# Weight sums staged in the tiles of later gated outputs, later landing estimates in the planner, gate scalings open to ScalarE, and earlier reloads of the first gated tiles

## The chip, the cores and the metric

The kernel runs on one core of a Trainium2 chip. The metric is device time in microseconds, from the first to the last work of one execution; the figure compared is the median of several runs. The engines are named as the profile names them: PE is TensorE (the matrix engine), PEld its weight loads, DVE is VectorE, ACT is ScalarE, POOL is GpSimd, and SP is the engine on whose queue nearly all transfers are issued.

## The reference

One layer of a mixer over 512 frames of 2048 features, all in float32. Both head groups read the same input through one projection; their gated outputs are concatenated, projected back, added to the input and normalised.

```python
proj = einsum('btd,dc->btc', h, w_in)                    # 512 x 2048 by 2048 x 8320
rw   = _token_shift(proj[..., :RWKV_COLS], shift_mu)     # y + mu * (y_prev - y)
hg   = proj[..., RWKV_COLS:]
# RWKV-7 group, 16 heads of 64
a = sigmoid(a0 + ad @ a_up)
k = k * (1.0 + (a - 1.0) * k_a)
o = _rwkv7_scan(r, decay, k, v, -kk, kk * a)             # a state 64 x 64 for each head
o_rwkv = (group_norm(o) + bonus) * silu(z_r)
# HGRN2 group, 8 heads of 128
log_f = logaddexp(log_lb, log1p(-lb) + log_sigmoid(f_raw))
k = (1.0 - lb) * sigmoid(-f_raw)
o_hgrn = rms_norm(_hgrn2_chunkwise(q, log_f, k, i)) * g_norm_w * silu(z_h)
y = einsum('btc,cd->btd', concatenate([o_rwkv, o_hgrn]), w_out)   # 512 x 2048 by 2048 x 2048
h = _layer_norm(ALPHA * h + y, ln_w, ln_b)
```

## The kernel before

**The large products.** A float32 factor is split into a rounded part and the rest (tiles xh and xl of the input, wh and wl of the weights). Each product of a 128x128 and a 128x512 tile is then three matmuls: high by high, high by low, low by high (`three`, L520). There are 3,852 of these matmuls; the text calls them large matmuls. Weights come in transfers of 128x1024 into tiles wr, two buffers of them; each half is split by ACT (wh, a rounding copy) and DVE (wl, the subtraction, L378), into three buffers. One such half serves 12 large matmuls of a projection.

**The projections.** `ORDER` lists 57 units of 48 large matmuls and two of 192 (w, k, r, v, z for the RWKV group, q, f, g, i for HGRN2). PE walks that list. Between its large matmuls the short matmuls of the heads are put in.

**The heads.** For each two RWKV heads' groups there is a preparation, an inversion of triangular 32x32 blocks (`rwkv_invert`, some 60 short DVE instructions and five long transposes on inv and big tiles), a fold, and a scan over eight chunks. In a scan step PE multiplies the state bd by q ("mix<-bd,q"), DVE subtracts the result from zz (L378), PE multiplies zz by q ("mix<-zz,q"), and DVE updates bd. A finished head gives a gated tile g; twelve of the sixteen are written to DRAM (spill), and pairs of them are read back and combined (`put_gated`, `token_sums`).

**The output product.** Its first 512 columns and its last 512 are computed directly; columns 512 to 1536 by seven products of half-size blocks instead of eight, which need sums of weight blocks (`weight_sums`, L1319) and sums over token halves of the gated tiles. The weight sums are made early: sixteen pieces of 128x1024 are read from w_all, four subtractions on DVE turn a piece into its four sums, and the result is written to sums_w in DRAM and read again near the end. Two threads do this, one with each of the two inv tiles. The inversion asks for both inv tiles too (`room(inv=2)`).

**What sets the order.** No order is written out by hand apart from `ORDER`. A planner (`Plan`, L91) keeps an estimated clock for each engine and for the transfers. It walks PE's large matmuls; after each (`pump`) it offers every thread its next step, and issues it if its operands are estimated to be there and its engine is near. What it issues is then the program order on that engine; on the chip each engine runs its own instructions strictly in that order and waits on semaphores. An estimate that is too early therefore costs a wait on the chip, with all that stands behind it on that engine. For a transfer `fetched` (L161) assumes that it lands 1.8 us after its bytes have passed. An operation with several ways (`Op`) is given to the engine that is estimated to end it first.

**Around the end.** `split_gated` splits a gated tile into gh and gl, in the buffers of xh and xl, which the last projection (z7) gives back a piece at a time; `reload` issues its read from spill first. `begin_out` is a hook that runs within z7: it reloads four tiles and, from the second quarter on, splits one in each quarter. `residual` reads the input rows (x_r), `fetch_norm` the weights of the last normalisation, `bring` the stored token sums, and `extra` opens two more buffers of two t tiles for weights.

## Time and profile before

| what | value |
|---|---|
| time, median of 3 runs | 1014.86 us (1014.38 to 1015.51) |
| the profiled execution: its own time | 1015.35 us |
| the profiled execution: span, first to last instruction | 1013.5 us |
| PE busy | 1005.8 us (99%), 7081 matmul records |
| PE weight loads busy | 830.8 us (82%) |
| DVE busy | 864.2 us (85%) |
| ACT busy | 507.0 us (50%) |
| POOL busy | 43.0 us (4%) |
| granted TensorE clock | 1.00 (2.4 GHz) in every slice |
| mean DMA rate | 160 GB/s, 349 GB/s in the first slice |

A matmul's end in the profile is modelled: a matmul of 128x512 is shown with 0.39 us, while the next one starts 0.23 us after it. So the busy share of PE is no measure of lost time. What shows lost time is the distance from one start to the next in the list of instructions in order of time, and the square brackets behind an instruction, which tell how long its engine sat idle before it and what ended that. The rows further below are of that kind. A label such as "main<-xl,wh" names the tile written and the tiles read, without buffer numbers.

### The profile page before, as it was taken

To read this page: it belongs to the slowest core of one execution; us is meant where nothing else is said; L and a number is where in the kernel's file an instruction comes from. 1 tells how busy PE (TensorE), PEld (TensorE's weight loads), DVE (VectorE), ACT (ScalarE), POOL (GpSimd) and SP (SyncE) were. 2 spreads that over 40 slices of the span, in tenths; PEclk is the share of its full clock that TensorE was granted. 3 is DMA by queue.
4 is the path that set the end of the run, shared out by engine and by line. 5 is a ranking of instruction groups with operands and counts; after the bars stand their busy time and mean duration, and the time that the engine had idled before them with its cause. 6 is when DMAs were issued, how large, how long until landed. Compare 5 with 4: busy or idle time off the path is not lost.

```text
span 1013.5 us, 18887 instructions
## 1 busy us (share of the span) xinstructions
PE 1005.8 (99%) x7081; PEld 830.8 (82%) x7081; DVE 864.2 (85%) x1894; ACT 507.0 (50%) x963; POOL 43.0 (4%) x78
## 2 busy tenths in 40 slices
PE   9999999999999999999999999999999999999997
PEld 8888888888888888888888888888888878888886
DVE  7688689967898998888989987888999887998867
ACT  5557335344646335535673456636343555466531
POOL 0000000000010001002000010020001001000001
PEclk9999999999999999999999999999999999999999
DMA  9666664443455453235555422346463248797633
GB/s 349 234 208 212 220 218 142 130 136 86 140 146 182 109 151 95 64 100 151 151 180 160 111 87 85 90 140 174 140 182 118 70 139 252 221 314 239 206 125 127
DMA packets 80492, 161.74 MB, mean 160 GB/s; under 512 B 11408, under 2 KB 38288, under 8 KB 80400
## 3 DMA queue, kind: packets, MB, share of 16 engines
q1 hardware_dynamic: 79968, 159.61, 51.2%
q8 instruction: 56, 0.92, 0.4%
q10 hardware_dynamic: 432, 0.92, 0.2%
q14 instruction: 36, 0.29, 0.1%
HBM read 130.48 MB, written 30.02 MB: 158 GB/s over the span
## 4 chain that ended last, share of the span: by engine, by line
PE 91%; DVE 4%; DMA 3%; issue 1%; SPq 1%; ACT 1%; DVEq 0%; ACTq 0%
PE main L525 69%; PE mix L354 9%; PE mix L525 8%; PE main L1390 3%; PE main L354 2%; DMA far<-ksq 1%; DVE wl L378 1%; DVE inv L378 1%; SPq L332 1%; DMA t<-w_all 1%; DVE t L378 1%; DVE xl L378 0%; DMA g<-x_r 0%; PE mix L1341 0%; DMA t<-far 0%
## 5 line engine op out<-in xcount | busy, mean ns | idle before, releaser
L525 PE MATMUL main<-xl,wh 128*128 128x512 f32 x848 | 333.2, 393 | 0.0
L525 PE MATMUL main<-xh,wl 128*128 128x512 f32 x848 | 333.1, 393 | 0.0
L525 PE MATMUL main<-xh,wh 128*128 128x512 f32 x848 | 332.9, 393 | 0.0
L368 ACT ACTIVATE wh<-wr 128x512 fp32r<-128x512 f32 x285 | 177.7, 627 | 166.3 <-PE main L525 120.0
L378 DVE TENSOR_TENSOR wl<-wr,wh 128x512 fp32r<-128x512 f32 x285 | 193.9, 681 | 28.8 <-ACT wh L368 24.8
L525 PEld LDWEIGHTS main<-xh,wl 128*128 128x128 f32 x848 | 159.3, 188 | 32.5
L525 PEld LDWEIGHTS main<-xl,wh 128*128 128x128 f32 x848 | 159.3, 188 | 32.4
L525 PEld LDWEIGHTS main<-xh,wh 128*128 128x128 f32 x848 | 159.3, 188 | 32.2
L525 PE MATMUL main<-wh,xh 128*128 128x512 f32 x194 | 76.2, 393 | 0.1
L378 DVE TENSOR_TENSOR inv<-inv 128x256 f32<-128x256 f32 (+10 forms) x184 | 64.5, 355 | 13.6 <-DMA inv<-w_all 10.1
L525 PE MATMUL main<-wh,xl 128*128 128x512 f32 x194 | 76.0, 392 | 0.0
L525 PE MATMUL main<-wl,xh 128*128 128x512 f32 x194 | 75.9, 391 | 0.0
L525 PEld LDWEIGHTS main<-wh,xh 128*128 128x128 f32 x194 | 36.4, 188 | 8.1 <-DVE t L391 0.5
L525 PEld LDWEIGHTS main<-wl,xh 128*128 128x128 f32 x194 | 36.4, 188 | 7.4
L525 PEld LDWEIGHTS main<-wh,xl 128*128 128x128 f32 x194 | 36.4, 188 | 7.3
L378 DVE TENSOR_TENSOR inv<-inv,inv 64x30 f32<-64x30 f32 (+14 forms) x120 | 38.5, 321 | 2.7
L368 ACT ACTIVATE t<-mix 64x128 f32<-64x128 f32 (+3 forms) x71 | 18.4, 262 | 41.3 <-DVE zz L378 23.9
L378 DVE TENSOR_TENSOR t<-t,tot 128x256 f32<-128x256 f32 x96 | 37.9, 416 | 0.3
L369 ACT ACTIVATE t<-main,om 128x512 f32<-128x512 f32 x33 | 22.2, 685 | 29.4 <-PE main L525 22.3
L391 DVE SCALAR_TENSOR_TENSOR bd<-mix,pc,bd 64x64 f32<-64x64 f32 x112 | 31.7, 283 | 5.3 <-PE mix L354 3.0
L368 ACT ACTIVATE q<-t 128x256 f32<-128x256 f32 (+1 forms) x51 | 21.9, 446 | 25.7 <-DVE t L378 25.5
L391 DVE SCALAR_TENSOR_TENSOR t<-main,pr,t 128x511 f32<-128x511 f32 x33 | 24.3, 744 | 5.8 <-ACT t L369 5.5
(320 smaller groups left out, 1607.7 us busy)
## 6 DMA issues: line engine op xcount, KB each, us to landing
wr<-w_all SPq DMA_DIRECT2D x142, 512.0 KB, 3.9
inv<-w_all SPq DMA_DIRECT2D x16, 512.0 KB, 5.0
sums_w<-inv SPq DMA_DIRECT2D x16, 512.0 KB, 5.1
q<-head SPq DMA_DIRECT2D x14, 448.0 KB, 5.6
far<-ksq SPq DMA_DIRECT2D x22, 256.0 KB, 4.2
t<-w_all SPq DMA_DIRECT2D x20, 256.0 KB, 4.9
t<-spill SPq DMA_DIRECT2D x17, 256.0 KB, 4.2
far<-q SPq DMA_DIRECT2D x8, 512.0 KB, 5.1
```

The source lines that it names most:

```text
L332: nc.sync.dma_start(o, i)
L354: return Op([("pe", cost, lambda: pe.matmul(o, l, r, start=start, stop=stop, **kw))], [l, r], [o], mode=("narrow", l.shape[0], 32 if m <= ...
L368: return "act", cost, lambda: sc_e.activation(o, i, f, scale=scale)
L369: return "act", cost, lambda: sc_e.activation(o, i, f, scale=scale, bias=bias)
L378: return dve_op([a, b], o, lambda: dve.tensor_tensor(o, a, b, f), base=base or 0.16 if o.shape[0] < P and size(o) == C and o.tensor.name i ...
L391: return dve_op([a, b], o, lambda: dve.scalar_tensor_tensor(o, a, s, b, f1, f2), per=0.00113, base=0.085 if o.shape[0] == P and size(o) > ...
L525: pe.matmul(ps, l, r, start=first and i == 0, stop=last and i == 2)
L1390: pe.matmul(pss[a], *ops, start=k == 0 and low == of == 0, stop=k == KT - 1 and low == 1)
```

## The change

The planner's function for transfers takes the delay as an argument, and six callers pass a larger one: 4.0 us for the reload of a stored gated tile that is to be combined, for the weight sums, for x_r and for the last normalisation's weights, 3.6 us for the reload of a gated tile before its split, 4.5 us for the stored token sums. The loads of weights into wr and into the t tiles keep 1.8 us. The planner also adds 0.09 us to PE's clock for a large matmul that follows a 128x128 one of the heads.

The weight sums move from one inv tile of 128x1024 for each of two threads to two g tiles of 128x512 each. A piece is read by two transfers of 128x512 instead of one of 128x1024, and written by two instead of one; the same four subtractions are done. The inv tiles are then free for the inversion from the start. The normalisation's weights come in eight transfers instead of four.

Three scalings by values of one per row (one of the RWKV preparation, two of the HGRN2 gates) may go to ACT as well as to DVE (`affine`). In the program, the eight of the preparation and eight of the sixteen of the gates do. A hook `ahead_of_out` reloads gated tiles within z6, one projection earlier than before, where four t tiles are free.

```diff
-    def fetched(self, tile, size):
+    def fetched(self, tile, size, late=1.8):
         self.clock["dma"] = max(self.clock["dma"], self.clock["sp"]) + size * 128 / 360e3
-        self.ready[tile.tensor.name] = (self.clock["dma"] + 1.8, "dma")
+        self.ready[tile.tensor.name] = (self.clock["dma"] + late, "dma")
...
+    def affine(o, a, s1, s2=0.0):
+        if isinstance(s2, float):
+            f = lambda: dve.tensor_scalar(o, a, s1, None, ALU.mult)
+            w = act_way(o, a, AF.Copy, s1)
+        else:
+            f = lambda: dve.tensor_scalar(o, a, s1, s2, ALU.mult, ALU.add)
+            w = act_way(o, a, AF.Identity, s1, s2)
+        return Op([w, ("dve", 0.07 + size(o) * banked(a), f)], [a], [o])
...
-            plan.clock["pe"] += n / 2400 + 0.0145 + plan.turn(("main",))
+            plan.clock["pe"] += n / 2400 + 0.0145 + plan.turn(("main",)) + (0.09 if plan.mode[0] == "whole" else 0.0)
...
-                    plan.fetched(r, 4 * T)
+                    plan.fetched(r, 4 * T, 4.0)
...
-        yield ts(a, a, hcol(HKA, p), hcol(HOKA, p), ALU.mult, ALU.add)
+        yield affine(a, a, hcol(HKA, p), hcol(HOKA, p))
...
-            yield ts(f, f, olb[:, h : h + 1], lbm[:, h : h + 1], ALU.mult, ALU.add)
-            yield ts(k, k, olb[:, h : h + 1], None, ALU.mult)
+            yield affine(f, f, olb[:, h : h + 1], lbm[:, h : h + 1])
+            yield affine(k, k, olb[:, h : h + 1])
...
     def weight_sums(first):
-        yield room(inv=1)
-        w = take("inv", [P, 4, QT // 2])
+        yield room(g=2)
+        ws = [take("g", [P, 2, QT // 2]) for _ in range(2)]
+        w = [w_[:, i] for w_ in ws for i in range(2)]
         for i in range(first, 2 * NPAIRS, 2):
             m, h = divmod(i, 2)
-            yield lambda: plan.clock["sp"] <= plan.clock["pe"] + 0.2
-            send(w, w_all[nsent + i].rearrange("p (a c) -> p a c", a=4))
-            plan.fetched(w, 4 * HALF)
+            cs = slice(h * QT // 2, (h + 1) * QT // 2)
+            raw = w_all[nsent + i].rearrange("p (a c) -> p a c", a=4)
+            for j, w_ in enumerate(ws):
+                yield lambda: plan.clock["sp"] <= plan.clock["pe"] + 0.2
+                send(w_, raw[:, 2 * j : 2 * j + 2])
+                plan.fetched(w_, 2 * HALF, 4.0)
             for o, a, b in ((0, 1, 0), (1, 3, 1), (3, 3, 0), (2, 2, 3)):
-                yield tt(w[:, o], w[:, a], w[:, b], ALU.subtract)
-            yield lambda: by_now(w)
-            yield lambda: plan.clock["sp"] <= plan.clock["pe"] + 0.2
-            send(sums_w[:, :, m, h * QT // 2 : (h + 1) * QT // 2].rearrange("a p c -> p a c"), w)
-            there = plan.busy[w.tensor.name] = (plan.clock["sp"] + 4.5, "dma")
-            yield lambda: there[0] <= plan.clock["pe"]
-        drop(w)
+                yield tt(w[o], w[a], w[b], ALU.subtract)
+            for j, w_ in enumerate(ws):
+                yield lambda: by_now(w_) and plan.clock["sp"] <= plan.clock["pe"] + 0.2
+                send(sums_w[2 * j : 2 * j + 2, :, m, cs].rearrange("a p c -> p a c"), w_)
+                plan.busy[w_.tensor.name] = (plan.clock["sp"] + 5.5, "dma")
+            there = plan.clock["sp"] + 5.5
+            yield lambda: there <= plan.clock["pe"]
+        drop(*ws)
...
                 send(gated[k], spill[SPILL.index(k)])
-                plan.fetched(gated[k], 4 * T)
+                plan.fetched(gated[k], 4 * T, 3.6)
...
         send(r, sums_a[m : m + some, i, :, half].rearrange("m p c -> p m c"))
-        plan.fetched(r, 2 * T * some)
+        plan.fetched(r, 2 * T * some, 4.5)
...
+    def ahead_of_out(j):
+        if plan.free("t", 4):
+            reload(min(len(asked) + 1, 4))
+
...
-            ps = proj(unit(), begin_out if (name, j) == ("z", NPAIR - 1) else None)
+            near = {("z", NPAIR - 1): begin_out, ("z", NPAIR - 2): ahead_of_out}
+            ps = proj(unit(), near.get((name, j)))
...
             send(xr, x_r[t, :, d * T : d * T + T])
-            plan.fetched(xr, 4 * T)
+            plan.fetched(xr, 4 * T, 4.0)
...
-        for d in range(4):
-            c = slice(d * T, d * T + T)
-            send(w[:, :, c], ln_wb[None, :, c].to_broadcast([P, 2, T]))
-            plan.fetched(w, 8 * T)
+        for d in range(8):
+            c = slice(d * T // 2, d * T // 2 + T // 2)
+            send(w[:, :, c], ln_wb[None, :, c].to_broadcast([P, 2, T // 2]))
+            plan.fetched(w, 4 * T, 4.0)
             now = plan.clock["pe"]
-            yield lambda: plan.clock["pe"] > now + 5.0
+            yield lambda: plan.clock["pe"] > now + 6.0
```

The first place is SP's queue around the start of z7. The reads of gated tiles are "t<-spill", the loads of weights "wr<-w_all". Before:

```order
L332 DMA wr_8569<-w_all 128x1024
L332 DMA wr_8681<-w_all 128x1024
L332 DMA wr_8753<-w_all 128x1024
L332 DMA t_8776<-spill 128x512
L332 DMA t_8778<-spill 128x512
L332 DMA t_8780<-spill 128x512
L332 DMA t_8782<-spill 128x512
L332 DMA t_8852<-spill 128x512
L332 DMA wr_8872<-w_all 128x1024
```

The same stretch of SP's queue in the changed program:

```order
L332 DMA wr_8570<-w_all 128x1024
L332 DMA wr_8663<-w_all 128x1024
L332 DMA t_8683<-spill 128x512
L332 DMA t_8715<-spill 128x512
L332 DMA wr_8747<-w_all 128x1024
L332 DMA t_8762<-spill 128x512
L332 DMA wr_8862<-w_all 128x1024
L332 DMA t_8883<-spill 128x512
L332 DMA t_8914<-spill 128x512
```

Five reads in a row have become two, one and two, with loads of weights between them, and the first two stand one load earlier.

The second place is SP's queue at the end of the first 512 output columns, where x_r and the t tiles of `extra` are loaded. Before:

```order
L332 DMA g_9527<-x_r 128x512
L332 DMA g_9533<-x_r 128x512
L332 DMA g_9550<-x_r 128x512
L332 DMA g_9557<-x_r 128x512
L332 DMA t_9553<-w_all 128x512
L332 DMA t_9554<-w_all 128x512
L332 DMA wr_9582<-w_all 128x1024
L332 DMA t_9574<-w_all 128x512
L332 DMA t_9575<-w_all 128x512
```

The same stretch in the changed program:

```order
L332 DMA g_9568<-x_r 128x512
L332 DMA g_9573<-x_r 128x512
L332 DMA g_9582<-x_r 128x512
L332 DMA g_9587<-x_r 128x512
L332 DMA t_9592<-w_all 128x512
L332 DMA t_9593<-w_all 128x512
L332 DMA t_9596<-w_all 128x512
L332 DMA t_9597<-w_all 128x512
L332 DMA wr_9618<-w_all 128x1024
```

The second pair of t tiles now stands ahead of the load into wr instead of behind it.

The third place is DVE's queue where the inversion of the first group begins (the transposes inv<-big). Before:

```order
L378 TENSOR_TENSOR wl_1682<-wr_1532,wh_1681 128x512
L378 TENSOR_TENSOR t_1016<-t_1016,tot_1326 128x16x16
L378 TENSOR_TENSOR tot_1325<-tot_1326 128x16
L427 COPY q_1320<-t_1016 128x8x32
L404 STREAM_TRANSPOSE inv_1698<-big_772 32x1024
L378 TENSOR_TENSOR wl_1711<-wr_1589,wh_1710 128x512
```

And in the changed program, where the instructions on g tiles are weight sums:

```order
L378 TENSOR_TENSOR g_271<-g_272,g_271 128x256
L378 TENSOR_TENSOR wl_1088<-wr_976,wh_1087 128x512
L414 STREAM_TRANSPOSE inv_1082<-big_765 32x1024
L378 TENSOR_TENSOR wl_1109<-wr_1019,wh_1108 128x512
L414 STREAM_TRANSPOSE inv_1082<-big_765 32x1024
L378 TENSOR_TENSOR wl_1126<-wr_1019,wh_1125 128x512
L378 TENSOR_TENSOR inv_1083<-inv_1082 64x30
L378 TENSOR_TENSOR inv_1082<-inv_1082,inv_1083 64x30
L378 TENSOR_TENSOR inv_1083<-inv_1082 64x58
L378 TENSOR_TENSOR inv_1082<-inv_1082,inv_1083 64x29x2
L378 TENSOR_TENSOR g_272<-g_272,g_271 128x256
```

The inversion of the first group begins 20 weights' halves earlier (its first transpose moves from ahead of large matmul 662 to ahead of 423), and weight sums stand within it and after it; before, the last of them stood ahead of it.

## Rows read from the trace of the kernel before

**Rows 1.** The chain that ended last, an undisturbed piece: start, duration, what.

```profile
57.20 16.11 PE main L525 x71
```

**Rows 2.** Instructions in order of time around 820 us: start, duration, instruction [idle before].

```profile
812.64 3.83 SPq L332 DMA_DIRECT2D t<-spill  x5
...
818.18 0.63 ACT L368 ACTIVATE xh<-t 128x512 fp32r<-128x512 f32 x1 [1.70 <-PE mix L354]
...
818.84 0.69 DVE L378 TENSOR_TENSOR xl<-t,xh 128x512 fp32r<-128x512 f32 x1 [1.33 <-ACT xh L368]
...
819.82 0.39 PE L525 MATMUL main<-xh,wl 128*128 128x512 f32 x1
...
820.90 0.47 DVE L378 TENSOR_TENSOR zz<-zz,mix 64x128 f32<-64x128 f32 x2
...
821.23 0.71 PE L354 MATMUL mix<-zz,q 128*128 128x128 f32 x4 [1.01 <-DVE zz L378]
```

**Rows 3.** The stored gated tiles' transfers between 800 and 895 us.

```profile
DMA to landing us min/median/max: 2.9/4.5/7.4
```

**Rows 4.** In order of time from 880 to 885 us.

```profile
880.75 0.69 DVE L391 SCALAR_TENSOR_TENSOR q<-g,main 128x512 f32<-128x512 f32 x1 [1.35 <-DMA g<-x_r]
...
882.78 0.33 SPq L332 DMA_DIRECT2D wr<-w_all  x1
...
883.20 0.86 SPq L332 DMA_DIRECT2D t<-w_all  x2
...
884.24 0.39 PE L525 MATMUL mix<-wh,xh 128*128 128x512 f32 x1
...
884.61 0.50 PE L525 MATMUL mix<-wl,xh 128*128 128x512 f32 x1
...
884.94 0.40 PE L525 MATMUL mix<-wh,xl 128*128 128x512 f32 x1
```

**Rows 5.** In order of time from 889 to 891 us.

```profile
889.12 0.63 ACT L368 ACTIVATE wh<-t 128x512 fp32r<-128x512 f32 x1 [1.74 <-DMA t<-w_all]
...
889.95 0.40 PE L525 MATMUL mix<-wh,xh 128*128 128x512 f32 x1
...
890.54 0.50 PE L525 MATMUL mix<-wl,xh 128*128 128x512 f32 x1 [0.19 <-DVE wl L378]
```

**Rows 6.** In order of time at 570 and at 830 us, PE alone.

```profile
569.81 0.39 PE L525 MATMUL main<-wl,xh 128*128 128x512 f32 x1
...
570.45 0.47 PE L354 MATMUL mix<-ksq,ones_r 128*128 128x512 f32 x1 [0.25 <-DVE ksq L378]
...
829.57 0.39 PE L525 MATMUL main<-wh,xl 128*128 128x512 f32 x1
...
830.02 0.50 PE L525 MATMUL main<-wh,xh 128*128 128x512 f32 x1
```

**Rows 7.** Costliest groups, shapes apart: busy us, mean ns | idle before.

```profile
L378 DVE TENSOR_TENSOR inv<-inv 128x256 f32<-128x256 f32 x64 | 26.0, 421 | 11.0 <-DMA inv<-w_all 10.1
...
L388 DVE TENSOR_SCALAR t<-t,half 128x512 f32<-128x512 f32 x8 | 4.3, 536 | 0.0
...
L369 ACT ACTIVATE t<-main,om 128x512 f32<-128x512 f32 x33 | 22.2, 685 | 29.4 <-PE main L525 22.3 <-PE main L1390 7.0
```

**Rows 8.** Transfers by line: count, size, median us to landing.

```profile
inv<-w_all SPq DMA_DIRECT2D x16, 512.0 KB, 5.0
...
t<-w_all SPq DMA_DIRECT2D x20, 256.0 KB, 4.9
...
g<-x_r SPq DMA_DIRECT2D x16, 256.0 KB, 5.6
```

**Rows 9.** Busy time by stretch: PE, PEld, DVE, ACT, POOL; clock, DMA.

```profile
160.00:200.00 40.00, 40.00 (x221) 32.91 (x220) 38.29 (x96) 16.33 (x35) 0.16 (x1) 1.00 0.51 149
```

**Rows 10.** Who waited for whom, whole span: total, times, longest (us).

```profile
DVE inv L378 <- DMA inv<-w_all: 10.1, 7, 3.3
```

**Rows 11.** One line's instructions, the long transposes: first and last start.

```profile
L404 DVE STREAM_TRANSPOSE inv<-big x8: 1962/2020/2042, 164.1 to 727.0; 32x1024 f32<-32x1024 f32 x8
```

## The prediction

> **What bounds the kernel now.** The page comes first. PE is busy for 1005.8 of 1013.5 us, but a matmul's end is modelled there, so this share can't say how much is lost. The chain of waits comes second: an undisturbed piece of it has 71 large matmuls in 16.11 us, 0.227 us each [rows 1]. 3,852 of them make 874 us; the rest of PE's time is the short matmuls of the heads and the two ends of the span. The reader is to see that PE is the bound from 5 us on, and that nothing else can set the time unless it makes PE wait. The third view is therefore the list of instructions in order of time, where a distance between two starts above 0.227 us, with no short matmul between, is lost time. I looked for all distances that stand out and found five places, worth 2.7 us together:
>
> - At 820 us PE starts a large matmul at 819.82 and the next instruction at 821.23 [rows 2]: 1.41 - 0.23 = 1.18 us lost. PE waited for zz from DVE. Five reads from spill were issued in a row from 812.64 on. ACT's split of the first one began only at 818.18 after 1.70 us idle; DVE's subtraction of that split stood idle 1.33 us for it, and zz was queued behind it until 820.90. The profile names PE as what ACT waited for. I take it for the transfer: 818.18 - 812.64 = 5.5 us, and such reads took 2.9 to 7.4 us there [rows 3].
> - At 884 us: 884.24 to 884.61 is 0.37, and the next distance is 0.33, so 0.14 + 0.10 = 0.24 us. DVE had stood 1.35 us for x_r at 880.75, and the weights' subtractions were queued behind that [rows 4].
> - At 890 us: 889.95 to 890.54 is 0.59, so 0.36 us, and 0.10 for the distance after it as above: 0.46 us. ACT had stood 1.74 us for a t tile of weights [rows 5]. That load had stood in SP's queue behind one into wr and was issued at 883.20 [rows 4].
> - At 570 and at 830 us: distances of 0.64 and 0.45 [rows 6], so 0.41 + 0.22 and 0.10 after each: 0.83 us, let us say 0.8.
>
> 1.18 + 0.24 + 0.46 + 0.8 = 2.7. So 2.7 us, 0.27%, is all that better order can return, and a change of 0.2% is 2.03 us, about what a measurement of this kernel can tell from no change.
>
> **The change part by part.** *What PE executes.* The order shows the same 3,852 large and 1,648 short matmuls on PE, in 124 separate groups of short ones instead of 122, and the same kinds of groups. Two more breaks cost at most two such distances after a break, 2 x 0.10 = 0.2 us [rows 4], and at least nothing, because the short matmuls themselves are the same; I take 0, as the 0.10 was read after a wait. The last 100 instructions of PE and DVE are of the same kinds in the same order, so the tail keeps its time.
>
> *Reload delay and the hook in z6.* The first two reads from spill now stand one load of weights earlier on SP, and the other three are spread among the loads. Between the load in front of which they stand and the first split on ACT lie three halves of weights, each good for 12 large matmuls: 3 x 12 x 0.227 = 8.2 us, against a landing of 4.5 us in the median and 7.4 at most [rows 1, 3]. The wait of 1.33 us on DVE goes, and with it 1.18 us on PE. What is late next there: DVE has the subtraction of the first split directly before zz again. By the order the split may begin when 12 matmuls of z7 are done; 0.63 on ACT and 0.69 on DVE take it 1.3 us further, with the two zz instructions (0.47) 1.8 us [rows 2]. PE needs zz after nine large matmuls and a pair of short ones, at 9 x 0.227 = 2.0 us plus that pair. It fits, with few tenths of a us to spare.
>
> *x_r taken to land 4.0 us after its bytes.* DVE's additions on x_r are placed later in its queue, and the weights' subtractions ahead of them. The planner had 1.8 and a transfer of 256 KB at 360 KB a us, 0.7, so 2.5 us; now 4.7; the rows have 5.6 in the median [rows 8]. Up to 0.9 us of the 1.35 can stay, and that is less than a split tile's lead of 12 x 0.227 = 2.7 us. I count the 0.24 as gone, and nothing as the other bound.
>
> *The second pair of t tiles.* It passes one load into wr in SP's queue. That load was issued at 882.78, the pair at 883.20, and with 0.43 for each issue the pair could now stand right behind the first pair, some 2 us earlier [rows 4]. ACT's wait was 1.74 us [rows 5], so 0.46 us go; the bound below is 0, if SP is held elsewhere. The load into wr comes 0.9 us later for it, under the cover of the other wr tile.
>
> *Weight sums in g tiles.* 64 subtractions of 421 ns stay, 27 us of DVE [rows 7]. 32 transfers become 64: 32 more issues of 0.43 us, 14 us of SP, spread over some 200 us. Each half waits on SP for its sums, and loads into wr are queued behind it; while one wr tile is read the other is loaded, and a tile lasts 24 large matmuls, 5.4 us. While that cover holds it costs nothing; without it, PE stands as long as SP did beyond it. The inversion of the first group, which began at 164.1 us [rows 11], begins 239 large matmuls earlier, 239 x 0.227 = 54 us, thus near 110 us. Nothing waits for it sooner: the fold that follows stands at large matmul 891 instead of 903. So it brings nothing to PE by itself.
>
> *Scalings on ACT.* Sixteen of 536 ns leave DVE, 8.6 us; ACT takes sixteen of about 685 ns (its nearest row with a factor per row), 11 us [rows 7]. DVE takes some short copies back. ACT is half idle, so at worst each holds a split of weights for 0.69 us, within the 2.7 us lead; at best DVE's freed time takes away the waits at 570 and 830 us. I count 0, between 0 and 0.8 us of gain.
>
> *The normalisation's weights* come in eight issues instead of four and are used 80 us later: nothing.
>
> **The sum.** 1.18 + 0.24 + 0.46 = 1.88 us. Of the profiled execution's own time, 1015.35 us (its span and 1.85 us around it), 1013.5 us are left. The median of the runs stands 0.49 us below that execution, so the forecast for it is 1014.86 - 1.9 = 1013.0 us, 0.18% less.
>
> **The rivals.**
>
> *All five waits go.* For it speaks that the planner's clock is nearer to the rows for six kinds of transfers and for PE's own turn, so DVE is held less in general. Against it: the waits at 570 and 830 us have no transfer of those kinds beside them. 1014.86 - 2.7 = 1012.2 us.
>
> *New waits as large as the old.* Nearly every engine's queue is in another order; the loads into wr, most of all transfers, keep their 1.8 us. Five places of thin margin can be five others. Net of 0.4 us: 1014.5 us.
>
> *Slower: DVE held within the inversion.* From 160 to 200 us DVE was busy for 38.29 of 40 us, with the inversion and no weight sums, and PE lost nothing [rows 9]. Now weight sums stand among the inversion's instructions. A sum that waits for its load holds DVE in order, and in so full a stretch nothing is left to catch up with: the weights' subtractions come late by as much, and PE stands. Such waits were 10.1 us in seven, 1.44 us each, the longest 3.3 [rows 10], all ahead of the inversion. Three pieces of sums fall into the inversion by the order. Three waits of 1.44 are 4.3 us: 1013.0 + 4.3 = 1017.3 us. It decides from waits of 3.9 us together on (1.9 gained and 2.0 lost). Against it: the sums are now taken to land at 4.7 us, near their 5.0 [rows 8].
>
> By the page "DMA: Bandwidth & Descriptors" of the Trainium skill (section "Anatomy of one DMA"), a transfer costs a fixed 2.0 us and its bytes at 436 KB a us, and its "Rules for kernel authors" ask for large transfers; halving the pieces then pays 2.0 us twice, and if the two parts came one after the other, three pieces would be late by 6 us and this rival would end near 1019 us. This trace speaks against that: 256 KB land in 4.9 us, issued in pairs, and 512 KB in 5.0 [rows 8], so the halves lie beside each other and I leave the rival its price by rows.
>
> **How the numbers follow.** The forecast has 0.46, all waits gone 0.20, as many new ones 0.19, the slower one 0.15. Faster by over 0.2% means under 1012.8 us: all of the second case and some 0.18 of the first, whose own range is 1012.2 to 1013.9; together 0.38. Slower means over 1016.9: the 0.15. The same: 0.47. The range runs from 1011.3 (all waits gone, and half a us of the spread of the runs shown, with small waits that I did not list) to 1016.8 us, where the smaller part of the slower case is in.
>
> **What would show it.** After the change, around z7, DVE's subtraction on xl should have no idle time before it and the zz matmuls should follow at 0.23 us; DVE should not stand for x_r when the first 512 columns end, nor ACT for a t tile of weights. The inversion's first transpose should begin near 110 us, with PE's starts 0.227 us apart beside it. The prediction is wrong if PE's distances between 105 and 165 us show waits of a us or more, or if the three places keep theirs.

## The result and the profile after

| | median | runs shown | ratio to before, 95% interval |
|---|---|---|---|
| before, same chip | 1015.18 us | 1014.38 to 1016.79 (4) | |
| changed | 1021.31 us | 1017.05 to 1022.90 (4) | 1.0053 [1.0034, 1.0072] |
| changed, measured again (e1) | 1023.08 us | 1020.40 to 1023.59 (5) | 1.0071 [1.0059, 1.0083] |

The change costs 6 to 8 us. The forecast was 1013.0 us in a range of 1011.3 to 1016.8: wrong by sign. The executions also lie further apart than those of before, so one trace isn't enough: the first trace is of the shortest execution (1017.05 us), that of e1 of one of 1020.40 us.

What was forecast for PE at the three places came true. In the first trace of the changed kernel, in order of time, DVE's subtraction of the reloaded tile has no idle time before it, and PE's next distance comes after 823.36 - 822.99 = 0.37 us, so 0.14 us are lost where it was 1.18 [rows 2]:

```profile
822.30 0.68 DVE L378 TENSOR_TENSOR xl<-t,xh 128x512 fp32r<-128x512 f32 x1
...
822.99 0.39 PE L535 MATMUL main<-xh,wl 128*128 128x512 f32 x1
...
823.36 0.71 PE L354 MATMUL mix<-zz,q 128*128 128x128 f32 x4
```

The signs that I had named for the other two came true in part: DVE still stands 0.39 us for x_r where it was 1.35 [rows 4], and ACT 1.16 us for a t tile where it was 1.74 [rows 5]. PE no longer stands for either:

```profile
883.03 0.69 DVE L401 SCALAR_TENSOR_TENSOR q<-g,main 128x512 f32<-128x512 f32 x1 [0.39 <-DMA g<-x_r]
...
886.93 1.99 ACT L368 ACTIVATE wh<-t 128x512 fp32r<-128x512 f32 x3 [1.16 <-DMA t<-w_all]
```

The losses are elsewhere. Here is the list of PE in the execution of e1, the changed kernel once more: every start with over 0.4 us idle before it, from 100 us on, and the start ahead of it. The first one has no releaser: "issue" is idle time in which PE waited for nothing that the profile shows. The group that it cuts in two takes 165.82 - 162.86 = 2.96 us to the next large matmul (next fence), where such a group alone takes 158.64 - 157.96 = 0.68, so 2.28 us are lost. The other distances lose 1.10, 1.42, 0.77 and 0.57 us (over 0.23 us behind a large matmul, 0.31 ahead of mix<-q,t), and 0.32 and 0.42 us more stand right behind 598 and at 531 us; 6.9 us together. Some 2.3 of the 2.7 us of before are gone, so 4.6 us are left; the two executions differ by 1020.40 - 1015.35 = 5.05 us, and the rest is in distances that lose 0.3 us or less.

```profile
165.58 0.31 PE L354 MATMUL mix<-inv,inv 32*32 32x32 f32 x11 [2.06 <-issue]
...
208.35 0.39 PE L535 MATMUL main<-xh,wl 128*128 128x512 f32 x1
209.67 0.47 PE L354 MATMUL mix<-ksq,ones_r 128*128 128x512 f32 x1 [0.94 <-DVE ksq L378]
...
573.41 0.39 PE L535 MATMUL main<-wh,xh 128*128 128x512 f32 x1
575.05 0.47 PE L354 MATMUL mix<-ksq,ones_r 128*128 128x512 f32 x1 [1.26 <-DVE ksq L378]
...
597.73 0.39 PE L535 MATMUL mix<-wl,xh 128*128 128x512 f32 x1
598.82 1.21 PE L354 MATMUL mix<-q,t 128*32 128x48 f32 x64 [0.70 <-DVE q L378]
...
871.23 0.39 PE L535 MATMUL main<-wh,xh 128*128 128x512 f32 x1
872.03 0.63 PE L359 MATMUL mix<-cst,t 128*128 128x128 f32 x4 [0.41 <-DVE t L378]
```

What the first stand is, is seen from what PE did before it (same trace). Three groups of 64 short matmuls stand within 6 us, the last two back to back, and PE stops within the third, after 53 of 64. (The trace has 3,229 records of short matmuls for the program's 1,648, so most leave two.)

```profile
157.96 0.75 PE L354 MATMUL mix<-big 32*32 32x32 f32 x64
158.64 0.50 PE L535 MATMUL main<-wh,xh 128*128 128x512 f32 x1
...
162.04 0.89 PE L354 MATMUL mix<-q,t 128*32 128x48 f32 x64
162.86 0.65 PE L354 MATMUL mix<-inv,inv 32*32 32x32 f32 x53
...
165.82 0.50 PE L535 MATMUL main<-wh,xl 128*128 128x512 f32 x1
```

In the kernel before, the two groups of the inversion (mix<-big and mix<-inv,inv) stood at 213 and 218 us, alone. They are 55 us earlier because the inversion is: its first transpose starts at 105.6 us, where it was 164.1 [rows 11], and I had forecast 110. That puts them among the three groups of mix<-q,t, which moved as well, but the other way: from 139, 147 and 156 us to 143, 162 and 174 us.

The page's section on queues has what runs out there:

```profile
q8 instruction: 56, 0.92, 0.4%
```

These are PE's instructions: 56 transfers of 16,384 bytes, one for every 250 or so of its 14,162 matmuls and weight loads. In large matmuls such a piece lasts some 28 us; 128 short matmuls and their weight loads use one up in 1.5 us (0.82 and 0.68 us for the two groups).

That PE waits for such a piece can be counted. With its waits on semaphores PE has 14,294 records, 917,504 / 14,294 = 64 bytes each, so 256 make a piece. From 20 us on, the traces of this case have six stands for 'issue' of 0.9 us or more, and all of them lie at the border of a piece: in e1, e4, e5, e6 and e14 PE stops after record 1,985, in e4 too, whose order is another, and a second time in e14, at 611 us, after record 8,897, which is 1,985 + 27 x 256. In all six PE goes on 1.2 to 1.4 us after the last transfer of that queue before it has ended (in e1 it runs from 163.22 to 164.14 us, and PE goes on at 165.58).

### The profile page after: what moved, and what is told of

Its sections match the earlier page's. It is cut to its first block, busy times and chain, and to the rows that moved or that the text cites. A ratio compares the mean times of both kernels' runs of the same rounds, so it can differ in the third digit from the quotient of the medians.

```text
span 1015.2 us, 18915 instructions
## 1 busy us (share of the span) xinstructions
PE 1006.5 (99%) x7081; PEld 831.8 (82%) x7081; DVE 861.7 (85%) x1894; ACT 512.8 (51%) x963; POOL 42.4 (4%) x78
## 4 chain that ended last, share of the span: by engine, by line
PE 92%; DVE 3%; DMA 2%; ACT 1%; issue 1%; SPq 0%; DVEq 0%; ACTq 0%
PE main L535 68%; PE mix L354 10%; PE mix L535 9%; PE main L1405 3%; PE main L354 2%; DMA q<-far 1%; DVE wl L378 1%; DMA g<-w_all 1%; PE mix L1356 0%; DMA wr<-w_all 0%; DVE t L378 0%; SPq L332 0%; DVE g L378 0%; DVE big L414 0%; DVE inv L378 0%
## 5 line engine op out<-in xcount | busy, mean ns | idle before, releaser
L535 PE MATMUL main<-wh,xh 128*128 128x512 f32 x168 | 66.1, 394 | 0.0
L535 PE MATMUL main<-wl,xh 128*128 128x512 f32 x168 | 65.6, 391 | 0.0
L535 PE MATMUL main<-wh,xl 128*128 128x512 f32 x168 | 65.6, 390 | 0.0
L378 DVE TENSOR_TENSOR inv<-inv 64x30 f32<-64x30 f32 (+14 forms) x120 | 38.3, 319 | 2.4
L535 PEld LDWEIGHTS main<-wh,xl 128*128 128x128 f32 x168 | 31.5, 188 | 6.6
L535 PEld LDWEIGHTS main<-wh,xh 128*128 128x128 f32 x168 | 31.5, 188 | 6.5
L535 PEld LDWEIGHTS main<-wl,xh 128*128 128x128 f32 x168 | 31.6, 188 | 6.3
L369 ACT ACTIVATE t<-main 128x512 f32<-128x512 f32 x31 | 18.1, 595 | 23.1 <-PE main L535 23.0
```

The source lines that it names most:

```text
L369: return "act", cost, lambda: sc_e.activation(o, i, f, scale=scale, bias=bias)
L378: return dve_op([a, b], o, lambda: dve.tensor_tensor(o, a, b, f), base=base or 0.16 if o.shape[0] < P and size(o) == C and o.tensor.name i ...
L535: pe.matmul(ps, l, r, start=first and i == 0, stop=last and i == 2)
```

## The experiments

The kernel before measured 1014.51 to 1015.28 us beside them, and each ratio is to that. Theories A to G are named in the expectations.

**e1_again** is the changed kernel, unedited; its result stands above.

> The changed kernel once more, with more executions. Known so far: its profiled execution took 1017.05 us at a granted clock of 1.000, three others took 1020.2 to 1022.9 at 0.998. Theory A (the sums' loads hold DVE and SP at 190 to 208 us, PE stands there, and the clock falls behind that stand): again 1020 to 1022 us in most executions, and a trace at 0.998 would show the clock under 1 right after 208 us. Theory B (the new order elsewhere: the waits at 572 and 596 us): the same times, the clock falls near 572 to 600 us. Theory C (the start of the span, where the first large matmuls stand 0.43 us apart): the clock is low within the first 10 us.

Theory C is dead: the clock is 1.00 from 4.1 us to PE's end in this trace. The waits of A and B are both there, but not the lower clock behind them, and the stand for instructions is there, which none of the three had.

**e2_no_loads** leaves out 28 loads of the weight sums. (With `real` false, `send` counts the transfer in the planner and issues none.)

```diff
...
-                send(w_, raw[:, 2 * j : 2 * j + 2])
+                send(w_, raw[:, 2 * j : 2 * j + 2], real=i == first)
```

> The changed kernel with 28 of the 32 loads of the weight sums left out (each thread loads its two tiles once and then computes on what is there, so the sums of the weights are wrong numbers); every other instruction on every engine keeps its place. Theory A: DVE no longer waits for g<-w_all, the distance of 1.27 us on PE at 208 us goes, the clock stays at 1.000, and the time is 1015 to 1016.5 us. Theory B: the waits at 572 and 596 us and the lower clock stay, 1019 to 1022 us. Theory C: the same as B, 1019 to 1022 us.

1019.50 us (1014.97 to 1021.10, 12 runs), 1.0036 [1.0025, 1.0048]: half of the loss is left. The wait at 208 us is gone, as A said; in this trace, of an execution of 1016.42 us, PE goes from 206.24 to 206.47 to 206.70 there. A loss of 1.50 us at 572 us stayed, as B said.

**e3_sums_inv** puts the old `weight_sums` back (diff: the function of before); **e4_sums_g_alone** puts the new one alone into the kernel before.

> The changed kernel with the weight sums put back: one inv tile of 128x1024 for each of the two threads, loads of 512 KB, taken to land 1.8 us after their bytes, all else of the change kept. Theory A: the time is that of the other edits, 1013 to 1015 us, with no wait over 1 us on PE near 208 us. Theory B: the other edits bring the waits, 1017 to 1022 us.

> The kernel before with the weight sums in g tiles alone (two tiles of 128x512 a thread, two loads and two stores a piece, taken to land 4.0 us after their bytes), nothing else of the change. Theory A: DVE waits for g<-w_all by 1.4 us somewhere behind 150 us, PE stands there by about a us, 1017 to 1022 us. Theory B: no slower than before, 1014 to 1016 us. Theory C: 1014 to 1016 us.

e3: 1015.78 us, 1.0011 [1.0002, 1.0020]. e4: 1019.91 us, 1.0048 [1.0036, 1.0060]. So by these two the change costs with the weight sums in g tiles and hardly without them; e8 and e10 below show that this can't be taken for the price of the g tiles themselves. In e3 the inversion begins at 164.5 us again. In e4's trace PE stands for 'issue' too, within the same two groups, which stand back to back the other way round: 0.91 us at 167.52. The largest of its other waits is one of 1.38 us at 864 us, which neither before nor the changed kernel has.

**e5_no_sums_dma** leaves out the transfers of the sums, **e6_no_subs** the subtractions.

```diff
...
-        return sums_w[kind, :, 2 * q : 2 * q + 2].rearrange("p k c -> p (k c)")
+        return w_all[nsent + q]
...
-                send(w_, raw[:, 2 * j : 2 * j + 2])
+                send(w_, raw[:, 2 * j : 2 * j + 2], real=i == first)
...
-                send(sums_w[2 * j : 2 * j + 2, :, m, cs].rearrange("a p c -> p a c"), w_)
+                send(sums_w[2 * j : 2 * j + 2, :, m, cs].rearrange("a p c -> p a c"), w_, real=False)
```

```diff
-                yield tt(w[o], w[a], w[b], ALU.subtract)
+                yield dve_op([w[a], w[b]], w[o], lambda: None, n=QT // 2)
```

> The changed kernel without the transfers of the weight sums: 28 of the 32 loads and all 32 stores are left out, and the products near the end read pieces of w_all in place of the stored sums (so the middle output columns are wrong numbers). The order on PE, DVE and ACT is the same instruction by instruction. What was learnt from the first four: the clock is 1.00 in all traces, so theory C is dead; in the longer execution of the changed kernel PE stood 2.06 us at 165 us for nothing the profile shows ('issue'), while the transfer of its next page of instructions began 4.8 us after PE had passed the page before. Theory D (pages of instructions queue behind the data of the weight sums, where short matmuls now stand close together): the stand at 165 us goes and the spread between executions shrinks; with the wait at 208 us gone too the time is 1016.5 to 1018.5 us, what is left being the waits at 572 and 598 us. Theory A alone (loads hold DVE and SP): no better than without the loads alone, 1019 to 1020 us.

> The changed kernel with the 64 subtractions of the weight sums left out (27 us of DVE work, wrong sums); all transfers stay, each store still behind its load, and the other instructions keep their order. Theory A (what holds PE at 208 us is DVE, in order behind a load): DVE no longer waits for g<-w_all, the wait at 208 us goes, 1018 to 1020 us. Theory D (instruction pages behind data): the stand at 165 us stays in most executions, so 1020 us or more.

e5: 1016.72 us (1015.35 to 1019.98, 11 runs), 1.0027 [1.0015, 1.0039]. e6: 1021.92 us, 1.0068 [1.0056, 1.0080]. In e6 DVE has no sums to wait with, and PE still lost 1.42 us at 211 us: theory A's mechanism, DVE held behind a load, falls. What PE waits for is at the other end of that chain: ACT's copy of the tile transposed through DRAM (q<-q), which ACT reaches on time in e2 (0.32 us idle) and late in e6; from e6's list:

```profile
206.02 1.06 ACT L368 ACTIVATE q<-q 128x1024 f32<-128x1024 f32 x1 [3.65 <-DMA q<-far]
```

In the changed kernel four loads of 256 KB for the sums stand between the write to far and its reads on SP, and e2, without them, has no wait there: the reads land late behind them. From the trace of e1:

```profile
190.81 0.43 SPq L332 DMA_DIRECT2D far<-q  x1
191.29 1.69 SPq L332 DMA_DIRECT2D g<-w_all  x2
193.84 0.33 SPq L332 DMA_DIRECT2D wr<-w_all  x1
194.21 0.91 SPq L332 DMA_DIRECT2D g<-w_all  x2
196.14 1.84 SPq L332 DMA_DIRECT2D q<-far  x4
```

Theory D fell in the form I gave it, though the median of e5 lies in its range. The trace of e5 is of its long kind, 1019.96 us, and has the stand without any transfer of the sums (columns by stretch: PE, PEld, DVE, ACT, POOL, clock, DMA share, GB/s):

```profile
160.00:162.00 2.00, 2.00 (x11) 1.54 (x9) 2.00 (x6) 1.46 (x4) 1.83 (x8) 1.00 0.04 14
162.00:164.00 2.00, 1.69 (x119) 1.31 (x118) 1.97 (x6) 0.00 (x0) 0.00 (x0) 1.00 0.04 8
164.00:166.00 2.00, 0.58 (x13) 0.50 (x13) 1.90 (x9) 0.23 (x1) 0.00 (x0) 1.00 0.84 244
166.00:168.00 2.00, 2.00 (x7) 1.61 (x6) 1.27 (x5) 1.90 (x5) 0.00 (x0) 0.64 0.09 27
168.00:170.00 2.00, 2.00 (x6) 1.53 (x5) 1.99 (x7) 1.44 (x3) 0.00 (x0) 0.51 0.00 0
```

The transfers are idle from 160 to 164 us (0.04), yet the piece of instructions arrives only there. It can be told from the border of the piece before, record 1,729 of PE. By the records of that queue the next transfer began 2.8 us after PE had passed it in e5 (162.69 us) and 3.5 us in e1, and 2.7, 3.5 and 2.9 us in e6, e14 and e4; in the two traces of this order without a stand (the first one of the changed kernel, and e2) it began within 0.4 us of it. (The 4.8 us of the expectation for e1 don't come out of the trace in this way.) Why it varies stays open. The transfers of the sums may have a part in it: four of e5's eleven executions are longer than 1017.1 us, where eight of the changed kernel's nine are; but e5 has no wait at 208 us either, so this isn't shown. The last two rows show a second price: behind the stand the granted clock is 1.2 GHz from 166.5 to 170.0 us, and e5's list shows eight large matmuls at 0.43 us each, 8 x 0.20 = 1.6 us:

```profile
165.42 0.31 PE L355 MATMUL mix<-inv,inv 32*32 32x32 f32 x11 [1.73 <-issue]
...
166.81 0.63 PE L536 MATMUL main<-wh,xh 128*128 128x512 f32 x1
167.23 0.63 PE L536 MATMUL main<-wl,xh 128*128 128x512 f32 x1
167.66 0.63 PE L536 MATMUL main<-wh,xl 128*128 128x512 f32 x1
```

The stand loses 1.9 us here, reckoned as in e1. Stand and clock are 1.9 + 1.6 = 3.5 us, and e5's executions lie in two heaps, seven at 1015.4 to 1016.9 us and three at 1020.0, with one between. Of the changed kernel itself no trace with the lower clock was taken; six of its nine executions show a mean clock of 0.997 or 0.998. But the longest of the nine (1023.59 us) shows 1.000, and so does one of e5's three long ones: that the clock makes the difference between long and longer executions isn't shown.

**e7_sums_later** has the edit below; **e8_inv_no_affine** has that of e3 and the three `ts` lines of before.

```diff
-                plan.fetched(w_, 2 * HALF, 4.0)
+                plan.fetched(w_, 2 * HALF, 6.0)
```

> The changed kernel with the loads of the weight sums taken to land 6.0 us after their bytes instead of 4.0; the planner makes a new order of it. Theory A: DVE's waits for g<-w_all go, 1016 to 1018 us. Theory D: the sums take even longer and overlap the short matmuls as much, 1019 to 1022 us. Theory E (the waits behind 500 us are accidents of the order and differ from order to order): waits of a us at other places than 572 and 598 us, none at these.

> The changed kernel with the weight sums put back into the inv tiles and the three scalings kept on DVE: what is left of the change are the landing delays, 0.09 us for PE and the earlier reloads. Theories A and D: as with the sums alone put back, 1014 to 1016 us, and the waits of the kernel before at 820 and 884 us gone. Theory E: the same within a us or two, with one or two waits at new places.

e7: 1069.75 us, 1.0542; e8: 1022.29 us, 1.0072 [1.0059, 1.0085]. The times that theories A and D gave were missed in both. In e7 the last scan is not done when its last projection ends; PE stands 17.42 us at 919.77 us for a split of the last gated tile, with the clock low for long stretches from 862 us on. In e8 PE stands 2.74 us at 865.11 us for a subtraction of weights, and the clock is 0.5 behind that again. Theory E holds in both: another order has other waits, here of 2.7 and 17.4 us.

**e9_short_apart** has the first edit, **e10_inv_held** the second.

```diff
-    BURST, WITHIN = 68, 3.0
+    BURST, WITHIN = 50, 3.0
```

```diff
     def rwkv_invert(SS, sc_all, far, keep):
+        if not held:
+            held.append(1)
+            yield lambda: plan.clock["pe"] > 158.0
         yield room(inv=2)
```

> The changed kernel with one number of the planner changed: at most 50 short matmuls of the 32-wide kinds within 3 us instead of 68, so that two groups of 32 never stand back to back (in the changed kernel mix<-q,t and mix<-inv,inv do at 163 us). Theory F (PE runs through short matmuls faster than its pages of instructions arrive, because the earlier inversion put its groups beside mix<-q,t): no stand by 'issue' at 160 to 170 us in the trace, no clock of 0.5 there, and the time falls by 2 to 3.6 us against the changed kernel, to 1018 to 1020 us, with the waits at 208 and 572 us left. Theory E (accidents of the order): anything from 1015 to 1023 us, and no relation to the stand.

> The changed kernel with the first inversion held back until the planner's clock is at 158 us, about where it began before; weight sums still in g tiles. The order differs from the changed kernel's only up to about 490 us, behind that it is the same instruction by instruction. Theory F: no stand by 'issue' at 165 us. Theory G (the loads of the weight sums push the reads q<-far of the next preparation back on SP and in the transfers, and PE waits for ksq at 208 us): the sums no longer meet that preparation beside the inversion, or still do; the wait at 208 us tells. Both together: what is left are the waits at 572 and 598 us, 2 to 3 us, 1015.5 to 1017.5 us. If the waits at 572 and 598 us are smaller too, they hang on the first half and are no matter of their own order.

e9: 1066.49 us, where 1018 to 1020 was expected; it is spoiled by the stand of e7 (17.49 us at 917.50). Between 160 and 170 us nothing stands and the clock is 1.00, as F says, but the piece of instructions was early in this trace (0.2 us after the border), as in the two of the changed order without a stand; so e9 does not test F. e10: 1014.74 us, 0.9996 [0.9988, 1.0005]: holding the first inversion back returns all of it, with the sums still in g tiles. Its trace has no stand at 165, the waits at 208 and 575 us are gone and 0.37 us is left of those at 598, though behind 515 us the order is that of the changed kernel. They hang on the place at 520 us where the orders still differ. There the changed kernel's SP has (trace of e1):

```profile
518.83 2.23 SPq L332 DMA_DIRECT2D q<-far  x3
521.16 0.38 SPq L332 DMA_DIRECT2D wr<-w_all  x1
521.59 0.43 SPq L332 DMA_DIRECT2D q<-far  x1
...
529.23 1.06 ACT L368 ACTIVATE q<-q 128x1024 f32<-128x1024 f32 x1 [3.71 <-DMA q<-far]
...
531.62 0.69 DVE L378 TENSOR_TENSOR wl<-wr,wh 128x512 fp32r<-128x512 f32 x1 [3.97 <-ACT wh L368]
```

and the kernel of e10 has the four reads together:

```profile
515.13 2.95 SPq L332 DMA_DIRECT2D q<-far  x4
518.18 0.38 SPq L332 DMA_DIRECT2D wr<-w_all  x1
...
522.93 1.06 ACT L368 ACTIVATE q<-q 128x1024 f32<-128x1024 f32 x1 [0.41 <-DMA q<-far]
```

One read behind a load of 512 KB makes ACT 3.71 us late and DVE 3.97. DVE is then busy for 14.42 of 15 us from 545 to 560 and 14.62 from 575 to 590, so it has little room to catch up; SP's loads into wr, which wait for DVE, are 5.3 us later than in e10 where PE is only 3.8 us later, and PE pays at 575 and again at 598 us. From 512 to 605 us the changed kernel's PE goes from 3.0 to 5.9 us behind that of e10, and the four losses of e1 there (0.42, 1.42, 0.77 and 0.32 us) make 2.9.

**e11_late_hook** and **e12_affine** are single parts in the kernel before: the two delays and the hook, and the three `affine` lines.

> The kernel before with only the 3.6 us for the reload of a gated tile before its split, the 4.0 us for x_r and the reload within z6. PE's order is that of the kernel before, instruction by instruction. By the steps of the prediction the waits at 820 us (1.18 us) and 884 us (0.24 us) go and nothing else changes: 1.4 us less than before, about 1013.2 us against 1014.5 to 1015.1 us. Rival: new waits for SP or DVE take their place, no difference.

> The kernel before with only the three scalings open to ACT. By the prediction 8.6 us of DVE go to ACT and PE gains between 0 and 0.8 us: 1014 to 1015 us. Theory E: one or two waits of a us at new places, 1016 to 1018 us.

e11: 1013.97 us, 0.9993 [0.9985, 1.0002]: 0.9 us less than before where 1.4 was expected, and not beyond what can be told. e12: 1020.79 us, 1.0062 [1.0048, 1.0076], with waits of 0.4 to 1.2 us at 338, 375, 749, 753, 759 and 828 us, none of which before has; theory E.

**e13_gap** has the first edit, **e14_reads_together** the second; **e15_hook_together** is the second one with the edits of e11 in the kernel before.

```diff
...
+        if not apart:
+            apart.append(1)
+            yield lambda: plan.short and plan.clock["pe"] > plan.short[-1] + 4.0
         pt, qs = yield from quarters(lambda i: (t22[:, i], yt[:, i]), a_i, tmp)
```

```diff
+        yield lambda: there[0] <= plan.clock["pe"] and plan.clock["sp"] <= plan.clock["pe"] + 0.2
         for b in range(rows):
-            yield lambda: there[0] <= plan.clock["pe"] and plan.clock["sp"] <= plan.clock["pe"] + 0.2
...
```

> The changed kernel with one wait for the planner alone: the second group of short matmuls of the first inversion (mix<-inv,inv) is issued 4 us after the group before it, and no longer right behind mix<-q,t. The inversion still begins early, the weight sums stay in g tiles; PE's order differs from the changed kernel's between 163 and about 515 us only. Theory F (instructions of two groups back to back use up a page before the next is there): no stand by 'issue' and no clock of 0.5 in the trace, 2 to 3.6 us less. Theory G (reads q<-far late on ACT): the wait at 208 us stays, about 1.1 us; at 520 us the four reads now stand ahead of the load into wr, so the waits at 531, 575 and 598 us go. Both: 1016 to 1017.5 us. If the early start of the inversion costs by itself, in another way, 1019 us or more.

> The changed kernel with the four reads of a tile transposed through DRAM (q<-far and the like) issued in one step, so that no load stands between them on SP. PE's order is that of the changed kernel up to 210 us, then another. Theory G: the late read at 520 us (three reads, a load into wr, the fourth read) is gone and with it PE's waits of 0.3 to 1.4 us at 531, 575 and 598 us; the stand at 165 us and the wait at 208 us stay, 1018 to 1020 us. Theory E (accidents of the order): another set of waits, anything from 1016 to 1024 us.

> The kernel before with the 3.6 us for the reload, the 4.0 us for x_r and the reload within z6 (1013.97 us in its own run, 0.07% less than before) and the four reads issued in one step. If late reads cost before's PE something at 570 us (0.83 us at 570 and 830 us), 1012.5 to 1013.5 us; theory E: 1014 to 1020 us.

e13: 1014.58 us, 0.9995 [0.9986, 1.0003], better than expected. The piece of instructions is as late as ever (it began at 163.62 us, 3.5 us after PE had passed the border), but PE has large matmuls to do and the next group comes at 169.64, so nothing stands. Here the piece is late and PE does not stand, as F says:

```profile
163.61 0.89 PE L354 MATMUL mix<-q,t 128*32 128x48 f32 x64
169.64 0.75 PE L354 MATMUL mix<-inv,inv 32*32 32x32 f32 x64
```

By that one group the planner also put two of four loads of the sums behind the reads at 194 us, and the four reads at 520 us together; the waits at 208 and 531 us go with it, and 0.29 and 0.37 us are left of those at 575 and 598. So e13 shows what hangs on the one place, not the price of the stand alone.

e14: 1023.85 us, 1.0084 [1.0070, 1.0098], 4 us over what theory G gave. The waits at 531, 575 and 598 us are gone, as theory G said, but the stand at 165 us, with the clock behind it, is there, PE idles 1.78 us at 212 us, and new ones came, one of them for 'issue' again (1.19 us at 611). e15: 1019.06 us, 1.0043 [1.0029, 1.0056]: theory E. No version is shown to beat the kernel before; e10, e11 and e13 can't be told from it.

## Why the prediction was wrong

*What was right.* PE is the bound, and what makes PE wait sets the time. The three treated waits went, the inversion began near where I said (105.6 us for 110), the subtractions kept their duration (419 ns). Of the 1.88 us of the sum 1.7 are there, by PE's distances in the first trace; e11, with the edits for two of the three places alone, could not be told from no gain.

*The step that failed.* Of the earlier inversion I wrote: "So it brings nothing to PE by itself." I had asked only who waits for its result, not what it is moved beside. With it go two groups of 64 short matmuls. The order showed the second back to back with mix<-q,t, and I had counted groups (124 for 122) and priced two more breaks at 0.2 us at most, "because the short matmuls themselves are the same". They are the same, but next to each other they use up PE's instructions before the next piece is there: 2.28 us in e1, 1.9 + 1.6 us with the clock in e5. My sum had nothing for this. The sign of being wrong that I had named, a wait of a us or more on PE between 105 and 165 us, came with it at 163.5 us, for a reason that was not among mine.

*A second step: "While that cover holds it costs nothing", of the transfers of the sums.* I looked at loads into wr behind them, which have a second tile as cover. The reads q<-far have none: ACT and DVE take them in order, and each of the two late ones was worth over 3 us on ACT and then 1.1 us (208) and some 2.9 us (531 to 598) on PE. Removing the loads alone removed the first (e2).

*The rival on the other side* had the right part of the change and the right direction, a time 4 us too low (1017.3), and the wrong place and mechanism. Waits of DVE for g<-w_all were there, 4.9 us in four in the first trace after the change, three at 195 to 201 us and one at 215 us, and the short DVE instructions of the first inversion ran from 111 to 149 us; but without any subtraction to wait with, PE lost as much (e6). Nor did the halved transfers make the sums later: 256 KB of them landed in 4.5 us in the median of the changed kernel, where 512 KB had taken 5.0 [rows 8].

*The 570 us wait* grew from 0.4 to 1.1 and 1.4 us instead of staying. *Scalings:* my 0 to 0.8 us of gain did not come in the kernel before (e12, 5.9 us slower), but e3, which has them, is 6.5 us faster than e8, which has not. So they have no price of their own that these runs could tell; what is measured is the order that the planner makes. My range took account of "new waits as large as the old"; e8, e12 and e15 show what another order costs: 4 to 8 us, up to three times the waits of before.

A page of the Trainium skill bears on the stand: "Runtime: NRT & Kernel Launch", section "Instruction fetch mechanics", says that an engine's instructions are streamed in blocks of 16 KiB and that crossing a block is "mostly hidden". The trace agrees on the block (0.92 MB in 56) and disagrees here on the hiding: PE sat idle for 0.9 to 2.1 us in the six stands. Had I read the order with that block in mind, the two groups back to back would have been a rival of their own.

## What to carry to other kernels

When an edit moves work to an earlier time, ask what it will then stand beside, on every queue: two groups of short matmuls that are harmless apart can outrun the transfers of PE's instructions, and a read that ACT and DVE take in order must not stand behind a large load. Where a planner makes the order, measure an edit against a few orders, or make one that differs in a single place and joins the old one again (e10, e13); otherwise the accident of the order, here 4 to 8 us, is taken for the edit. Executions that suddenly lie further apart can be a sign of a wait that only just happens, as the stand at 165 us was there in one of the two traces of the same program and not in the other.

## What was not expected of the hardware

Behind a stand of PE of 1.6 to 1.9 us idle (e5, e6, e14 at 165 us) and of 2.7 us (e8 at 865 us) the granted clock was 1.2 GHz for 3.4 us and large matmuls came every 0.43 us; behind the 2.06 us of e1 it stayed at 2.4 GHz. The transfer of a piece of PE's instructions began up to 3.5 us after PE had passed the border of the piece before, once with the transfers idle ahead of it (e5), and PE went on 1.2 to 1.4 us after its end.
